# Transposing activations by VectorE blocks and DRAM instead of by TensorE, in a two-block transformer kernel

## The chip, the cores and the metric

The kernel runs as one program on 1 core of a Trainium2 chip. The metric is device time of one execution in microseconds (us). Before the change three timed runs gave a median of 2368.16 us (2367.35 to 2370.7). The profile is of one further execution of the same program.

## The reference

Two transformer blocks in a row over 256 tokens of width 2048, all in float32. The first has differential attention, an indexed sparse attention and a gated feed-forward layer; the second has latent attention beside a gated convolution. What matters here:

```python
# first block, feed-forward (D_FF = 5632)
ff = (jax.nn.silu(h @ w_gate) * (h @ w_up)) @ w_down

# second block
proj = h @ w_in_2      # split into q_a, c_kv, k_rope, z_mla, c_in, b_gate, c_gate, z_conv, g_mla, g_conv
attn = attn * jax.nn.silu(z_mla)
y_mla = attn @ w_o_mla
u = c_gate * c_in
conv = sum(conv_w[k] * u_pad[:, k:k + s] for k in range(3))       # along the tokens
y_conv = (b_gate * conv * jax.nn.silu(z_conv)) @ w_o_conv
merged = jax.nn.sigmoid(g_mla) * y_mla + jax.nn.sigmoid(g_conv) * y_conv
out = merged @ w_out
```

Each product that is multiplied by a further matrix (the feed-forward product, the gated attention, the gated convolution and the merged sum) comes out of TensorE with tokens on the partitions. The next matmul needs it with channels on the partitions, so it has to be transposed; the convolution runs along the tokens and is computed on the transposed `u`.

## The kernel before, in words

Tokens are two tiles of 128 (t = 0, 1). A weight matrix is taken in groups of up to 512 columns (`Grp`), a group in units of two 128-row pieces (`kc`). Every float32 operand is split exactly in two parts (hi and lo), and TensorE adds three products per piece and token tile: hi by wh, hi by wl, lo by wh (line 65 records each matmul). A group over 16 pieces is 96 matmuls of 128x512.

Weights come by SyncE (SP) in loads of 1 MB, one load for two units, into four buffers `raw`. For each unit ScalarE writes `wh` (line 286) and VectorE writes `wl` (line 287); both have four buffers (`N_SPLIT`), and a unit is split at most three units ahead of the matmuls (`LOOK`). A buffer of `raw` is free again when both of its units are split, and the next load is issued right behind that split.

The order on every engine is the order in which the Python program emits instructions; each engine runs its own list in that order and stops at the first instruction whose inputs are not there. When the last matmul of a group for one t is emitted, `spawn` starts a generator `post_...`, which empties the PSUM bank. A generator gives up control with `yield d` and is taken up again when the program's own clock, which `PE.matmul` and `PE.transpose` advance, has gone on by d us (4.84 where nothing is given); that clock is a means of placing instructions and no measurement.

For a transpose, `quad_transpose` emits four TensorE transposes of 128x128 into one PSUM bank (line 70), and `put_quad` then writes the hi part with ScalarE (line 549) and the lo part with VectorE (line 550). It is used behind the feed-forward product (`post_up`, tile `act`), for `u` (`post_cgate`), for the gated convolution (`post_bgate`, tile `m`), for the gated attention (`post_z`, tiles `at`) and for the merged sum (`post_omla`, tiles `thm`). Each goes once per group and token tile.

The framework gives every DMA one of eight completion semaphores in turn (`DMAHW0` to `DMAHW7`); before SP issues a DMA it waits until the DMA eight places earlier has landed, where that is not known already.

Of the kernel before, what the change touches and what calls it, by code (L numbers as in the profile page):

```python
# [9 lines left out]
F32 = mybir.dt.float32  # L10
# [3 lines left out]
AF = mybir.ActivationFunctionType  # L14
# [3 lines left out]
P = 128  # L18
# [21 lines left out]
def kernel(ctx: ExitStack, tc: tile.TileContext, a, freq, out):  # L40
    nc = tc.nc
# [10 lines left out]
    drp = ctx.enter_context(tc.tile_pool(name="drp", bufs=1, space=bass.MemoryType.DRAM))  # L52
    ctx.enter_context(tc.manual_schedule())

    V, A, G = nc.vector, nc.scalar, nc.gpsimd
# [15 lines left out]

    T = PE

    # ------------------------------------------------------------------ storage
    slots = deque(range(14))
    slot_of = {}

# [12 lines left out]
    def wtile(shape=(P, 512), dt=F32, tag="w", bufs=4, name="w"):  # L90
        return wk.tile(list(shape), dt, name=name, tag=tag, bufs=bufs)
# [27 lines left out]
    def sc_bank():  # L119
        return psx.tile([P, 512], F32, name="sc", tag="sc", bufs=2)  # L120

    # ------------------------------------------------------------------ driver
    bg = []
    H = {}

# [246 lines left out]
                t = tt  # L372
            stages[-j](items[i])

    # ------------------------------------------------------------------ constants
    v1 = wtile(tag="P", bufs=4, name="v1")
    v1 = v1[:, :P]
    rows = lambda v, n: v.rearrange("o (r c) -> (o r) c", c=P)[:n]
# [30 lines left out]
    pb = tp_bank()  # L409
# [94 lines left out]
        V.tensor_scalar(nlam, nlam, 0.2, None, op0=OP.subtract)  # L504


    # ------------------------------------------------------------------ helpers
    def rstd_of(ssq, n, width, name="rstd"):
        k = ssq.shape[1]
        v = small(k, name + "v")  # L510
# [10 lines left out]
    def quad_transpose(src, pb=None):  # L521
        pb = pb if pb is not None else tp_bank()
        n = src.shape[1] // P
        for j in range(n):
            T.transpose(pb[:, j * P:(j + 1) * P], src[:, j * P:(j + 1) * P], ident)
        return pb[:, :n * P].rearrange("p (c q) -> p c q", q=P)
# [16 lines left out]
    def put_quad(pair, q, t, src, scale=None):  # L543
        hi, lo = pair
        k = 4 * q
        h = hi[k // 8][:, k % 8:k % 8 + 4, t * P:(t + 1) * P]
        l = lo[k // 8][:, k % 8:k % 8 + 4, t * P:(t + 1) * P]
        if scale is None:
            A.activation(h, src, AF.Copy)
            V.tensor_sub(l, src, h)  # L550
        else:
            A.activation(h, src, AF.Copy, scale=scale)
            V.scalar_tensor_tensor(l, src, scale, h, op0=OP.mult, op1=OP.subtract)

    # ------------------------------------------------------------------ modulation
    def ada_item(load, use, after=lambda: None):
        return {"kind": "ada", "item": {"kind": "ada", "load": load, "use": use}, "after": after}

# [3 lines left out]
    hid = {}  # L562
# [154 lines left out]
                set_state("ada_free", True)  # L717
        return gen

    # ------------------------------------------------------------------ first norm  # L720
    ssx = cst.tile([P, 2, 4], F32, name="ssx")
    first = ada_chunk(0)
    firsts = []
# [7 lines left out]
    for t in range(2):  # L731
# [5 lines left out]
        r = rstd_of(sum4(ssx[:, t, :]), 1, D)  # L737
        for q in range(4):
            xs = x_t[t][:, 512 * q:512 * (q + 1)]
            V.tensor_scalar(xs, xs, r, None, op0=OP.mult)  # L740
            pb = quad_transpose(xs)
            d = nT[q // 2][:, 4 * (q % 2):4 * (q % 2) + 4, t * P:(t + 1) * P]
# [6 lines left out]
    free("x0", "x1", "ada0", "ada1", "ada2", "ada3")  # L749
    hid["hi"], hid["lo"] = [big("h1h0", dt=R32), None], [big("h1l0", dt=R32), None]  # L750

    # ------------------------------------------------------------------ w_in of the first block
    acc = {}
    for q in range(2):
        acc["A", q] = big(f"accA{q}", (P, 2, 2, 512))
# [12 lines left out]
    w_in = a["w_in"][0]  # L768
# [26 lines left out]
            s += g.steps()  # L795
        return s

    # index scores and the selection of keys
    iws = cst.tile([P, 2, 16], F32, name="iws")

    def idx_gen():
# [310 lines left out]
    sd.insert(nd, call(start_diff))  # L1112
    steps += merge(sd, gate_a + shift_f)

    # ------------------------------------------------------------------ output of the attention
    mix_hi = lambda kc, t: (hid["mh%d" % (kc // 8)][:, kc % 8, t * P:(t + 1) * P],
                            hid["ml%d" % (kc // 8)][:, kc % 8, t * P:(t + 1) * P])
    w_o = a["w_o"][0]
# [91 lines left out]
    def after_o():  # L1210
        free("mh0", "ml0", "mh1", "ml1")

    # ------------------------------------------------------------------ feed-forward
    DFF = 5632
    w_gate, w_up, w_down = a["w_gate"][0], a["w_up"][0], a["w_down"][0]
    lhs2 = lambda kc, t: hilo_lhs(*hid["h2"])(kc, t)
# [4 lines left out]
    def post_gate(g):  # L1221
        def post(t, ps):
            sil[t] = hold("sil")
            A.activation(sil[t], ps, AF.Silu)
            yield 0
        return post

    def post_up(g, q):
        def post(t, ps):
            w = wtile(name="act")  # L1230
            V.tensor_mul(w, ps, sil[t])
            yield
            put_quad(hid["act"], q, t, quad_transpose(w))
        return post

    def act_alloc():
# [62 lines left out]
    for p, (g0, ng) in enumerate(parts):  # L1299
        if p == 0:  # L1300
            fsteps.append(call(after_o))
        fsteps.append(call(act_alloc))
        for g in range(g0, g0 + ng):
            if g == 1:
                fsteps.append(call(rel_mo))
            for nm, w, post in (("gate", w_gate, post_gate(g)), ("up", w_up, post_up(g, g - g0))):
                fsteps += Grp(f"{nm}{g}", w, 512 * g, 512, range(16), lhs2, post,
                              need=lambda ks, t: [f"h2.{t}.{k // 4}" for k in ks],
                              begin=2 if nm + str(g) == "gate0" else 1).steps()
        for g in range(4):  # L1310
            post = post_down(g, p) if p < 2 else post_norm_in(ffacc, ssf, g, "Gf", fin_f)

            def need(ks, t, p=p, g0=g0):
                r = [f"up{k // 4}.{t}" for k in ks]
                return r + (["ada5"] if p == 2 else [])
            fsteps += Grp(f"down{p}_{g}", w_down, 512 * g, 512, range(4 * g0, 4 * (g0 + ng)), lhs_act(p),
                          post, need=need, end=3 if (p, g) == (2, 3) else 1).steps()
# [2 lines left out]

    steps += fsteps[nf:]

    # ------------------------------------------------------------------ second block
    w_in2 = a["w_in_2"]
    lhs3 = lambda kc, t: hilo_lhs(*hid["h3"])(kc, t)
    need3 = lambda ks, t: [f"h3.{t}.{k // 4}" for k in ks]
# [58 lines left out]
    steps += Grp("ck0", w_in2, 512, 288, range(16), lhs3, post_ck0).steps()  # L1385
    steps += Grp("ck1", w_in2, 800, 288, range(16), lhs3, post_ck1).steps()

    # gated convolution
    C_IN, B_GATE, C_GATE, Z_CONV = 3136, 5184, 7232, 9280
    G_MLA, G_CONV, Z_MLA = 11328, 13376, 1088  # L1390
    uT = {}
# [10 lines left out]
    def post_cgate(g):  # L1402
        def post(t, ps):
            w = wtile(name="u")
            V.scalar_tensor_tensor(w, ps, r3[:, t, 0:1], sil[t], op0=OP.mult, op1=OP.mult)
            yield
            if g not in uT:
                uT[g] = big(f"uT{g}", (P, 2, 4, 256))
            u = uT[g]
            A.activation(u[:, 0, :, t * P:(t + 1) * P], quad_transpose(w), AF.Copy)  # L1410
            yield
            if t == 1:
                for j in range(4):
                    k = 4 * g + j
                    V.tensor_scalar(u[:, 1, j, :], u[:, 0, j, :], col2[:, 48 + k:49 + k], None, op0=OP.mult)
                    V.scalar_tensor_tensor(u[:, 1, j, 1:256], u[:, 0, j, 0:255], col2[:, 32 + k:33 + k],
                                           u[:, 1, j, 1:256], op0=OP.mult, op1=OP.add)
                    V.scalar_tensor_tensor(u[:, 1, j, 2:256], u[:, 0, j, 0:254], col2[:, 16 + k:17 + k],
                                           u[:, 1, j, 2:256], op0=OP.mult, op1=OP.add)
                    yield  # L1420
        return post
# [6 lines left out]
    def post_bgate(g):  # L1428
        def post(t, ps):
            w = wtile(name="m")  # L1430
            V.scalar_tensor_tensor(w, ps, r3[:, t, 0:1], sil[t], op0=OP.mult, op1=OP.mult)
            yield
            while not done(f"cgate{g}.0", f"cgate{g}.1"):
                yield POLL
            pb = quad_transpose(w)
            y = wtile(name="yc")
            y3 = y.rearrange("p (c q) -> p c q", q=P)
            V.tensor_mul(y3, pb, uT[g][:, 1, :, t * P:(t + 1) * P])
            put_quad(hid["y"], g, t, y3)
            yield 0  # L1440
            if t == 1:
                free(f"uT{g}")
        return post
# [8 lines left out]
    yc = [None, None]  # L1452
# [14 lines left out]
        steps += Grp(f"oconv{g}", a["w_o_conv_2"], 512 * g, 512, range(16), lhs_y, post_oconv(g),  # L1467
                     need=lambda ks, t: [f"bgate{k // 4}.{t}" for k in ks]).steps()

    # latent attention  # L1470
    knT, vt, qnT = [None, None], [None, None], [None, None]

    def kv_alloc():
# [140 lines left out]
    def post_z(g):  # L1614
        def post(t, ps):
            th = wtile(name="thz")
            A.activation(th, ps, AF.Tanh, scale=r3[:, t, 1:2])
            V.scalar_tensor_tensor(th, th, 1.0, ps, op0=OP.add, op1=OP.mult)
            yield 0
            if "att" not in hid:  # L1620
                while not done("mla"):
                    yield POLL
                if "att" not in hid:
                    hid["att"] = mk_pair("att")
            d = at[t][:, 512 * g:512 * (g + 1)]
            V.scalar_tensor_tensor(d, d, r3[:, t, 1:2], th, op0=OP.mult, op1=OP.mult)
            yield
            put_quad(hid["att"], g, t, quad_transpose(d))
        return post

    gsteps = []
# [29 lines left out]
    def post_omla(g):  # L1661
        def post(t, ps):
            d = thm[t][:, 512 * g:512 * (g + 1)]
            V.scalar_tensor_tensor(d, d, 1.0, ps, op0=OP.add, op1=OP.mult)
            V.tensor_add(d, d, yc[t][:, 512 * g:512 * (g + 1)])
            yield
            put_quad(hid["mer"], g, t, quad_transpose(d), 0.5)
        return post

    lhs_att = lambda kc, t: hilo_lhs(*hid["att"])(kc, t)  # L1670
# [2 lines left out]
    for g in range(4):  # L1673
        steps += Grp(f"omla{g}", a["w_o_mla_2"], 512 * g, 512, range(16), lhs_att, post_omla(g)).steps()

    # output projection
    ot = [None, None]
    x2 = [None, None]
    ssz = cst.tile([P, 2, 4], F32, name="ssz")
# [72 lines left out]
```

## Time and profile before

| | us |
|---|---|
| timed runs, median (lowest to highest) | 2368.16 (2367.35 to 2370.7) |
| profiled execution, span from the first to the last instruction | 2365.9 |
| TensorE matmul busy | 2315.8 (98%) |
| VectorE busy | 1306.1 (55%) |
| ScalarE busy | 1069.0 (45%) |
| bytes moved | 506.57 MB, 214 GB/s over the span |

The profiled execution's span lies 2.3 us under the median of the timed runs; what lies around the span is within that difference. A span is cut into 40 equal slices on the page, and a digit gives a slice's busy share in tenths. "busy" of TensorE's matmuls is modelled from their starts, so that a stream of them shows as 100% while each is listed with a duration longer than its distance to the next. The name before `<-` is the tile that is written, the names behind it are those that are read.

### The profile page before, as it was taken

How to read it: one execution, taken by the hardware profiler on the slowest of the kernel's cores; microseconds unless marked ns; L12 is line 12 of the kernel's file. 1: busy time of each engine (PE TensorE's matmuls, PEld its weight loads, DVE VectorE, ACT ScalarE, POOL GpSimd, SP SyncE). 2: the span in 40 equal slices, each digit the busy share in tenths (PEclk: the TensorE clock that was granted, in tenths of full speed). 3: DMA queues.
4: the chain of work that ended last, by engine and by line, in shares of the span. 5: the costliest groups of instructions: out<-in, count | busy, mean ns of one | idle time of the engine just before them, and what ended most of it. 6: DMA issues, size and time to landing. Idle time of an engine off the chain costs nothing.

```text
span 2365.9 us, 27898 instructions
## 1 busy us (share of the span) xinstructions
PE 2315.8 (98%) x11044; PEld 1842.3 (78%) x11044; DVE 1306.1 (55%) x1710; ACT 1069.0 (45%) x1503; POOL 96.8 (4%) x117
## 2 busy tenths in 40 slices
PE   7999999999999999999998999999999999999998
PEld 5666666677887888888887888888888988888887
DVE  3656756556664444554556655555544654554554
ACT  4434345546444444434444644444445544444443
POOL 1311011010000000000001000000000000000000
PEclk9999999999999999999999999999999999999999
DMA  9996888957775556556554665565565553565563
GB/s 302 330 320 237 318 309 301 318 209 277 242 261 191 191 192 195 179 196 195 186 188 144 220 195 190 179 200 188 179 204 161 168 171 125 172 219 196 187 204 125
DMA packets 237619, 506.57 MB, mean 214 GB/s; under 512 B 9288, under 2 KB 31984, under 8 KB 228400
## 3 DMA queue, kind: packets, MB, share of 16 engines
q1 hardware_dynamic: 235392, 496.14, 62.3%
q0 software_dynamic: 1872, 8.58, 1.1%
q8 instruction: 86, 1.41, 0.2%
q14 instruction: 45, 0.37, 0.0%
q10 hardware_dynamic: 224, 0.07, 0.0%
HBM read 500.56 MB, written 4.19 MB: 213 GB/s over the span
## 4 chain that ended last, share of the span: by engine, by line
PE 75%; DVE 1%; ACT 1%; issue 1%; POOL 0%; DVEq 0%; POOLq 0%; ACTq 0%
PE mm L65 71%; PE tp L70 1%; PE sc L65 1%; PE tp L65 1%; PE tpb L70 1%; DVE wl L287 0%; DVE xr L1155 0%; ACT h3h L1163 0%; DVE h3l L1166 0%; POOL rstd L513 0%; ACT wh L286 0%; ACT junk L1178 0%; DVE ot L1705 0%; ACT hm L1277 0%; DVE hm L1273 0%
## 5 line engine op out<-in xcount | busy, mean ns | idle before, releaser
L287 DVE TENSOR_TENSOR wl<-raw,wh 128x1024 fp32r<-128x1024 f32 (+3 forms) x723 | 871.9, 1212 | 766.5 <-ACT wh L286 760.4
L286 ACT ACTIVATE wh<-raw 128x1024 fp32r<-128x1024 f32 (+3 forms) x723 | 745.9, 1038 | 696.4 <-PE mm L65 686.3
L65 PE MATMUL mm<-wh,h3h 128*128 128x512 f32 (+1 forms) x992 | 387.1, 390 | 1.7 <-ACT h3h L1163 1.2
L65 PE MATMUL mm<-wl,h3h 128*128 128x512 f32 (+1 forms) x992 | 380.7, 384 | 0.4 <-DVE wl L287 0.4
L65 PE MATMUL mm<-wh,h3l 128*128 128x512 f32 (+1 forms) x992 | 381.0, 384 | 0.0
L65 PE MATMUL mm<-wh,h2h 128*128 128x512 f32 x704 | 276.3, 393 | 0.0
L65 PE MATMUL mm<-wl,h2h 128*128 128x512 f32 x704 | 274.6, 390 | 0.9 <-DVE wl L287 0.9
L65 PE MATMUL mm<-wh,h2l 128*128 128x512 f32 x704 | 274.7, 390 | 0.0
L65 PEld LDWEIGHTS mm<-wh,h3h 128*128 128x128 f32 x992 | 186.7, 188 | 37.8 <-ACT h3h L1163 1.6
L65 PEld LDWEIGHTS mm<-wh,h3l 128*128 128x128 f32 x992 | 186.5, 188 | 37.4 <-DVE h3l L1166 0.4
L65 PEld LDWEIGHTS mm<-wl,h3h 128*128 128x128 f32 x992 | 186.8, 188 | 34.8 <-DVE wl L287 0.6
L65 PE MATMUL mm<-wh,h1h 128*128 128x512 f32 (+2 forms) x384 | 154.0, 401 | 3.4 <-ACT wh L286 2.5
L65 PEld LDWEIGHTS mm<-wl,h2h 128*128 128x128 f32 x704 | 132.5, 188 | 28.1 <-DVE wl L287 1.2
L65 PEld LDWEIGHTS mm<-wh,h2h 128*128 128x128 f32 x704 | 132.5, 188 | 27.7 <-issue 0.8
L65 PEld LDWEIGHTS mm<-wh,h2l 128*128 128x128 f32 x704 | 132.4, 188 | 27.6
L65 PE MATMUL mm<-wl,h1h 128*128 128x512 f32 (+2 forms) x384 | 142.7, 372 | 7.8 <-DVE wl L287 7.8
L65 PE MATMUL mm<-wh,h1l 128*128 128x512 f32 (+2 forms) x384 | 142.0, 370 | 1.9 <-DVE h1l L627 1.9
L65 PE MATMUL mm<-wh,acth 128*128 128x512 f32 x352 | 139.3, 396 | 0.0
L65 PE MATMUL mm<-wh,actl 128*128 128x512 f32 x352 | 137.1, 390 | 0.0
L65 PE MATMUL mm<-wl,acth 128*128 128x512 f32 x352 | 137.0, 389 | 0.0
L65 PEld LDWEIGHTS mm<-wh,h1h 128*128 128x128 f32 x384 | 72.8, 190 | 55.7 <-issue 26.7
L65 PEld LDWEIGHTS mm<-wl,h1h 128*128 128x128 f32 x384 | 72.9, 190 | 21.2 <-DVE wl L287 10.9
(412 smaller groups left out, 2777.7 us busy)
## 6 DMA issues: line engine op xcount, KB each, us to landing
raw<-in_w_in_dram SPq DMA_DIRECT2D x134, 1024.0 KB, 5.2
raw<-in_w_ada_dram SPq DMA_DIRECT2D x47, 1024.0 KB, 4.9
raw<-in_w_gate_dram SPq DMA_DIRECT2D x44, 1024.0 KB, 5.3
raw<-in_w_up_dram SPq DMA_DIRECT2D x44, 1024.0 KB, 5.2
raw<-in_w_down_dram SPq DMA_DIRECT2D x44, 1024.0 KB, 5.1
raw<-in_w_ada_dram SPq DMA_DIRECT2D x36, 512.0 KB, 8.9
rawb<-in_w_ada_dram SPq DMA_DIRECT2D x17, 1024.0 KB, 6.5
raw<-in_w_o_conv_dram SPq DMA_DIRECT2D x16, 1024.0 KB, 5.1
```

Of the source, the lines that this page charges most:

```text
L65: return nc.tensor.matmul(o, l, r, **kw)
L70: return nc.tensor.transpose(o, i, idn)
L286: A.activation(wh[:, :m, :g.n], src, AF.Copy)
L287: V.tensor_sub(wl[:, :m, :g.n], src, wh[:, :m, :g.n])
```

## The change

A helper `flip_quad` takes the place of `quad_transpose` in 21 groups for both token tiles, 42 times: 8 of the 11 feed-forward groups (all but the last of each of the three parts), the four `u` groups, three of four `m` groups, three of four `at` groups and three of four `thm` groups. In each, VectorE transposes the 128x512 tile within 32x32 blocks into `scr`; four DMAs, one for each 32 partitions, write `scr` to a DRAM buffer in runs of 32 elements (128 bytes); one DMA reads the buffer back with 128 contiguous elements (512 bytes) per run, channels on the partitions. The result `fm` (or `uT` itself) lies in SBUF, and `put_quad` reads it there. All these DMAs are issued by SP. The generator gives up control for 2 us behind the block transpose, and for 8 us (`FLIP`) behind the writes and again behind the read.

```diff
+    FLIP = 8.0
+    n_flip = [0]
+
+    def flip_quad(src, dst=None):
+        n_flip[0] += 1
+        dr = drp.tile([P, 512], F32, name=f"flip{n_flip[0]}")
+        scr = wtile(tag="PT", bufs=2, name="scr")
+        V.transpose(scr, src)
+        yield 2.0
+        for i in range(4):
+            d = bass.AP(tensor=dr.tensor, offset=dr.offset + 32 * i, ap=[[P, 32], [32 * P, 16], [1, 32]])
+            nc.sync.dma_start(d, scr[32 * i:32 * i + 32].rearrange("p (b r) -> p b r", r=32))
+        yield FLIP
+        if dst is None:
+            dst = wtile(tag="P", bufs=4, name="fm").rearrange("p (c q) -> p c q", q=P)
+        s = bass.AP(tensor=dr.tensor, offset=dr.offset, ap=[[P, P], [P * P, 4], [1, P]])
+        nc.sync.dma_start(dst, s)
+        yield FLIP
+        return dst
...
-    def post_up(g, q):
+    def post_up(g, q, last):
         def post(t, ps):
             w = wtile(name="act")
             V.tensor_mul(w, ps, sil[t])
-            yield
-            put_quad(hid["act"], q, t, quad_transpose(w))
+            if q < last:
+                m3 = yield from flip_quad(w)
+            else:
+                yield
+                m3 = quad_transpose(w)
+            put_quad(hid["act"], q, t, m3)
         return post
...
             u = uT[g]
-            A.activation(u[:, 0, :, t * P:(t + 1) * P], quad_transpose(w), AF.Copy)
-            yield
+            yield from flip_quad(w, u[:, 0, :, t * P:(t + 1) * P])
...
-            pb = quad_transpose(w)
-            y = wtile(name="yc")
-            y3 = y.rearrange("p (c q) -> p c q", q=P)
-            V.tensor_mul(y3, pb, uT[g][:, 1, :, t * P:(t + 1) * P])
+            if g < 3:
+                y3 = yield from flip_quad(w)
+                V.tensor_mul(y3, y3, uT[g][:, 1, :, t * P:(t + 1) * P])
+            else:
+                pb = quad_transpose(w)
+                y = wtile(name="yc")
+                y3 = y.rearrange("p (c q) -> p c q", q=P)
+                V.tensor_mul(y3, pb, uT[g][:, 1, :, t * P:(t + 1) * P])
```

`post_z` (for g of 1 to 3) and `post_omla` (for g of 0 to 2) get the same two branches as `post_up`.

SyncE at the end of the feed-forward group up4, before the change: only weight loads follow one another, each waiting for the split that frees its buffer (`DVE_49`).

```order
L262 DMA raw_6750<-in_w_gate_dram 128x4x512 [waits DMAHW5_49,DVE_49]
L262 DMA raw_6784<-in_w_up_dram 128x4x512 [waits DMAHW6_49,DVE_49]
L262 DMA raw_6817<-in_w_up_dram 128x4x512 [waits DMAHW7_49,DVE_49]
L262 DMA raw_6872<-in_w_up_dram 128x4x512 [waits DMAHW0_49,DVE_49]
L262 DMA raw_6906<-in_w_up_dram 128x4x512 [waits DMAHW1_49,DVE_49]
```

SyncE at the same place after the change (`flip7` is the DRAM buffer of t = 0, `flip8` that of t = 1, `scr` the block-transposed tile, `fm` the tile read back):

```order
L262 DMA raw_6808<-in_w_up_dram 128x4x512 [waits DMAHW4_49,DVE_49]
L262 DMA raw_6847<-in_w_up_dram 128x4x512 [waits DMAHW5_49,DVE_49]
L566 DMA flip7_6822<-scr_6823 32x16x32 x4
L566 DMA flip8_6833<-scr_6834 32x16x32 [waits DMAHW6_49]
L566 DMA flip8_6833<-scr_6834 32x16x32 [waits DMAHW7_49]
L566 DMA flip8_6833<-scr_6834 32x16x32 [waits DMAHW0_49]
L566 DMA flip8_6833<-scr_6834 32x16x32 [waits DMAHW1_49]
L262 DMA raw_6896<-in_w_up_dram 128x4x512 [waits DMAHW2_49,DVE_49]
L571 DMA fm_6904<-flip7_6822 128x4x128 [waits DMAHW5_49,DMAHW4_49,DMAHW3_49]
L571 DMA fm_6916<-flip8_6833 128x4x128 [waits DMAHW6_49,DMAHW7_49,DMAHW1_49,DMAHW0_49]
L262 DMA raw_6934<-in_w_up_dram 128x4x512 [waits DVE_49]
```

Ten DMAs have come between three weight loads. The four writes of `flip8` wait for the four weight loads before them, the last of these for `raw_6847`, which SP has just issued. Each read waits for the writes of its own buffer, and the load `raw_6934` stands behind both reads.

ScalarE at the same place before the change: the two copies of the transposed product, each waiting for TensorE, stand among the splits.

```order
L286 ACTIVATE wh_6792<-raw_6675 128x1024 [waits DMAHW7_49,DVE_49,PE_49]
L286 ACTIVATE wh_6813<-raw_6675 128x1024 [waits DVE_49,PE_49]
L549 ACTIVATE acth0_4641<-tp_6832 128x4x128 [waits PE_49]
L286 ACTIVATE wh_6845<-raw_6716 128x1024 [waits DMAHW0_49,DVE_49]
L549 ACTIVATE acth0_4641<-tp_6849 128x4x128 [waits PE_49]
L286 ACTIVATE wh_6868<-raw_6716 128x1024 [waits DVE_49]
```

ScalarE after the change, from the same split on (`wh_6843` is now what `wh_6813` was, the second unit of its load):

```order
L286 ACTIVATE wh_6843<-raw_6699 128x1024 [waits DVE_49,PE_49]
L286 ACTIVATE wh_6876<-raw_6740 128x1024 [waits DMAHW6_49,DVE_49,PE_49]
L286 ACTIVATE wh_6892<-raw_6740 128x1024 [waits DVE_49,PE_49]
L286 ACTIVATE wh_6912<-raw_6774 128x1024 [waits DMAHW7_49,DVE_49,PE_49]
L286 ACTIVATE wh_6930<-raw_6774 128x1024 [waits DVE_49,PE_49]
L286 ACTIVATE wh_6948<-raw_6808 128x1024 [waits DMAHW0_49,DVE_49,PE_49]
L286 ACTIVATE wh_6964<-raw_6808 128x1024 [waits DVE_49,PE_49]
L549 ACTIVATE acth0_4641<-fm_6904 128x4x128 [waits DMAHW3_49]
L549 ACTIVATE acth0_4641<-fm_6916 128x4x128 [waits DMAHW4_49]
L286 ACTIVATE wh_6980<-raw_6847 128x1024 [waits DMAHW1_49,DVE_49,PE_49]
```

The copies stand six splits later than before, and wait for the landing of the two reads instead of for TensorE.

## Rows read from the trace of the kernel before

**Rows 1.** The page, sections 1 and 2: busy us (share) xinstructions; digits are tenths per slice.
```profile
PE 2315.8 (98%) x11044; PEld 1842.3 (78%) x11044; DVE 1306.1 (55%) x1710; ACT 1069.0 (45%) x1503; POOL 96.8 (4%) x117
...
PEclk9999999999999999999999999999999999999999
DMA  9996888957775556556554665565565553565563
```

**Rows 2.** Busy time by stretch: PE, PEld, DVE, ACT, POOL, granted clock, DMA share, GB/s.
```profile
590.00:710.00 120.00, 120.00 (x542) 99.40 (x542) 77.63 (x64) 51.82 (x55) 0.00 (x0) 1.00 0.73 252
710.00:1230.00 520.00, 520.00 (x2322) 428.22 (x2321) 254.85 (x229) 219.83 (x230) 0.00 (x0) 1.00 0.58 191
1380.00:1720.00 340.00, 340.00 (x1533) 281.63 (x1532) 190.13 (x203) 145.93 (x152) 0.00 (x0) 1.00 0.58 189
2030.00:2110.00 80.00, 80.00 (x366) 66.26 (x365) 47.88 (x49) 37.50 (x42) 1.12 (x2) 1.00 0.63 212
2180.00:2260.00 80.00, 80.00 (x366) 66.28 (x365) 45.65 (x46) 33.83 (x36) 0.37 (x1) 1.00 0.57 187
```

**Rows 3.** TensorE in order of time around one pair: start, duration, instruction.
```profile
909.02 0.39 PE L65 MATMUL mm<-wh,h2h 128*128 128x512 f32 x1
909.25 0.39 PE L65 MATMUL mm<-wl,h2h 128*128 128x512 f32 x1
909.48 0.40 PE L65 MATMUL mm<-wh,h2l 128*128 128x512 f32 x1
909.71 0.60 PE L70 MATMUL tpb<-ident,act 128*128 128x128 f32 x4
910.07 0.47 PE L65 MATMUL mm<-wh,h2h 128*128 128x512 f32 x1
910.38 0.39 PE L65 MATMUL mm<-wl,h2h 128*128 128x512 f32 x1
910.61 0.40 PE L65 MATMUL mm<-wh,h2l 128*128 128x512 f32 x1
```

**Rows 4.** Instructions on tile act: count, duration min/median/max, first and last start.
```profile
L70 PE MATMUL tp<-ident,act x72: 270/272/275, 595.5 to 1221.2; 128*128 128x128 f32 x72
...
L70 PE MATMUL tpb<-ident,act x16: 270/272/275, 909.7 to 1176.8; 128*128 128x128 f32 x16
```

**Rows 5.** ScalarE in order of time around group up4; in brackets idle before, and releaser.
```profile
861.36 1.06 ACT L286 ACTIVATE wh<-raw 128x1024 fp32r<-128x1024 f32 x1 [1.66 <-PE mm L65]
865.88 0.60 ACT L549 ACTIVATE acth<-tp 128x512 fp32r<-128x512 f32 x1 [3.47 <-PE tp L70]
...
870.46 1.06 ACT L286 ACTIVATE wh<-raw 128x1024 fp32r<-128x1024 f32 x1 [1.21 <-PE mm L65]
873.18 1.06 ACT L286 ACTIVATE wh<-raw 128x1024 fp32r<-128x1024 f32 x1 [1.66 <-PE mm L65]
```

**Rows 6.** VectorE in order of time, same place.
```profile
860.87 1.28 DVE L1231 TENSOR_TENSOR act<-mm,sil 128x512 f32<-128x512 f32 x2
862.45 1.23 DVE L287 TENSOR_TENSOR wl<-raw,wh 128x1024 fp32r<-128x1024 f32 x1 [0.30 <-ACT wh L286]
```

**Rows 7.** VectorE groups by shape: count, busy us, mean ns, idle before.
```profile
L550 DVE TENSOR_TENSOR actl<-tp,acth 128x512 fp32r<-128x512 f32 x18 | 12.4, 687 | 21.7 <-ACT acth L549 21.7
L550 DVE TENSOR_TENSOR yl<-yc,yh 128x512 fp32r<-128x512 f32 x8 | 5.5, 692 | 5.6 <-ACT yh L549 5.6
L1514 DVE COPY qrT<-tp 128x128 f32<-128x128 f32 x11 | 2.9, 281 | 0.0
L287 DVE TENSOR_TENSOR wl<-raw,wh 128x1024 fp32r<-128x1024 f32 x677 | 833.3, 1236 | 739.0 <-ACT wh L286 733.0 <-PE mm L65 4.3
```

**Rows 8.** SyncE's waits, whole span: us in total, times, longest.
```profile
SPq L262 <- DVE wl L287: 1593.1, 323, 14.3
```

**Rows 9.** DMA issues: count, KB each, median us to landing.
```profile
raw<-in_w_up_dram SPq DMA_DIRECT2D x44, 1024.0 KB, 5.2
out_dram<-ot SPq DMA_DIRECT2D x8, 256.0 KB, 2.1
```

**Rows 10.** The page, section 3, whole span: packets, MB, share of 16 engines.
```profile
q1 hardware_dynamic: 235392, 496.14, 62.3%
```

**Rows 11.** The same of 0 to 20 us: ScalarE's small loads.
```profile
q10 hardware_dynamic: 224, 0.07, 1.4%
```

**Rows 12.** SyncE's issue of one weight load: start, duration.
```profile
858.26 0.37 SPq L262 DMA_DIRECT2D raw<-in_w_up_dram  x1
```

More of the change, by code (lines that the diff above doesn't have):

```diff
@@ L1305 @@
                 fsteps.append(call(rel_mo))
-            for nm, w, post in (("gate", w_gate, post_gate(g)), ("up", w_up, post_up(g, g - g0))):
+            for nm, w, post in (("gate", w_gate, post_gate(g)), ("up", w_up, post_up(g, g - g0, ng - 1))):
                 fsteps += Grp(f"{nm}{g}", w, 512 * g, 512, range(16), lhs2, post,
@@ L1626, in post @@
             V.scalar_tensor_tensor(d, d, r3[:, t, 1:2], th, op0=OP.mult, op1=OP.mult)
-            yield
-            put_quad(hid["att"], g, t, quad_transpose(d))
+            if g:
+                m3 = yield from flip_quad(d)
+            else:
+                yield
+                m3 = quad_transpose(d)
+            put_quad(hid["att"], g, t, m3)
         return post
@@ L1665, in post @@
             V.tensor_add(d, d, yc[t][:, 512 * g:512 * (g + 1)])
-            yield
-            put_quad(hid["mer"], g, t, quad_transpose(d), 0.5)
+            if g < 3:
+                m3 = yield from flip_quad(d)
+            else:
+                yield
+                m3 = quad_transpose(d)
+            put_quad(hid["mer"], g, t, m3, 0.5)
         return post
```

## The prediction

> **What bounds the kernel now.** I read the page's busy shares first: TensorE 98%, the next engine 55%, the granted clock at full speed in all 40 slices [rows 1]. A share over the span hides stages, so I asked for the stretches in which the 42 transposes of the change lie. In all five TensorE is busy for the whole stretch (520.00 of 520 us, 340.00 of 340 us and so on), at a granted clock of 1.00, the level of 2.4 GHz, while VectorE is at 49 to 65%, ScalarE at 42 to 47% and the DMA engines at 0.57 to 0.73 [rows 2]. There TensorE sets the end, and nothing else is near it. SyncE waits for VectorE's splits to free a weight buffer, 323 times for 1593.1 us [rows 8]: weights wait for buffers, not buffers for weights. ScalarE's splits wait for TensorE in turn [rows 5], which closes the loop: TensorE is the pacemaker, and the engines behind it have room.
>
> **What goes from TensorE.** 42 quads of transposes, 168 instructions. Their listed duration, 272 ns each [rows 4], is not the price, because TensorE overlaps them. The price is read from starts. In a stream of matmuls one starts every 0.227 us (909.02, 909.25, 909.48). From 909.48 the third matmul further on would start at 909.48 + 3 x 0.227 = 910.16; with the quad between it starts at 910.61 [rows 3]. One quad costs 0.45 us, and 42 cost 18.9 us. All 42 lie in stretches in which TensorE never rests, so the whole sum is on the path. From the same rows, the bounds of a quad: 0.60 us (the quad's own listed time) and 0.36 us (910.07 less 909.71, without the slower restart), so 15 to 25 us for all; I take 0.45.
>
> **What comes on VectorE.** 42 block transposes of 128x512 from SBUF. The trace has none. Bounds: 0.28 us (copy of 128x128) and 1.24 us (two-input operation of 128x1024) [rows 7]; I take 0.7, as the two-input operations of 128x512 have. That makes 29 us on an engine that idles 739 us before the wl splits alone [rows 7]. The lo parts are now read from SBUF instead of PSUM: 692 ns against 687 [rows 7], nothing. On the path this counts only if a wl comes late. TensorE uses a unit three units after its buffer is freed: a unit is 2.72 us (870.46 to 873.18), so 8.2 us later, and the split takes 1.06 us on ScalarE and 1.23 on VectorE [rows 5, 6]. That leaves 5.8 us of room, and the added 1.4 us per pair fit. The cover is real: in this kernel ScalarE is already held 3.47 us at each first quad [rows 5], and TensorE does not rest there [rows 2].
>
> **What comes on SyncE and DMA.** Per pair (t = 0 and 1) eight writes and two reads, 210 issues in all at 0.37 us [rows 12]: 3.7 us per pair, in an interval of 5.4 us between two loads. Packets per pair: 8 x 512 of 128 bytes and 2 x 512 of 512 bytes. No row shows packets of 128 bytes, or a write in such runs. Bounds: a packet of 2 KB takes 0.623 x 16 x 2365.9 / 235392 us = 100 ns [rows 10], so 6 ns if only bytes count and 100 ns if only packets count. The nearest row has 300 bytes in the mean: 0.014 x 16 x 20 / 224 us = 20 ns [rows 11]. I take 20: on each of 16 engines 256 x 20 = 5.1 us for the writes and 64 x 20 = 1.3 us for the reads. The Trainium skill speaks against the change here ("DMA: Bandwidth & Descriptors", Specifications): runs under 512 bytes do not reach line rate, since the engine reads, modifies and writes. If that doubles the write, an estimate by that page, it is 40 ns and 10.2 us per pair; no run so far shows it, and by the following working the sum would not change.
>
> **Is the round trip in time?** This is where the forecast stands or falls, since ScalarE works in order and `acth<-fm` stands in front of the next split. I follow up4 on the old trace. The products are made from 860.87 to 862.15 [rows 6]; with two block transposes the next wl ends near 864.8, and then SP issues `raw_6847`, which lands at 870.0 (5.2 us [rows 9]). The first four writes queue behind it. The fourth write of `flip8` may only be issued once that load has landed, 870. The load's own data are through by about 868, then 5.1 us of writes: 873 to 874, and landed near 875. `raw_6896` follows at 870.5, behind the writes, its data (512 packets of 2 KB, 3.2 us) done by 877; the second read follows at 875, its data done by 878 and landed near 879. ScalarE, after six more splits of 2.72 us from 861.36, comes to the copy at 878.7. So it is held some 0.3 us, of 5.8 that are free. Price if the cover is gone: every microsecond of hold beyond 5.8 is one of TensorE, per pair. That happens from 5.5 us more on 256 packets, 41 ns a packet. In the convolution `u` is transposed one yield later and read by VectorE; by the same steps the reads land about 5 us before their use. The weight loads: `raw_6896` is half a microsecond late, `raw_6934` waits for the second read until 875.4 and would have been issued at about 875.7 anyway. The four buffers hold some 15 us of work beyond that, so this costs nothing.
>
> DMA share: 8 loads per 43.5 us (two groups of 96 x 0.227) keep the engines at 0.58; a pair adds 6.4 us, 0.15. In the at and thm stretches a pair comes every 21.8 us, adding 0.29 to 0.57 or 0.63 [rows 2]: 0.92 at most, for three groups in a row. In the first stretch (0.73) it becomes 0.88. Under 1 everywhere.
>
> **Sum.** 18.9 us off a span of 2365.9 gives 2347.0; with the 2.3 us by which the median of the runs shown exceeds that span, 2349.3 us.
>
> **Rivals.**
>
> *Held copies.* Packets near 43 ns, or landings of the writes some 6 us longer than I have: ScalarE holds each of the 14 tight pairs (8 feed-forward, 3 at, 3 thm) about half a microsecond beyond its room, 7 us in all: 2356. For it: my margin is a few microseconds of queueing that I stacked by hand. Against it: in the convolution the room is larger, and a hold of 3.47 us shows no cost now.
>
> *No change.* The time given up by TensorE is taken by the next bound at once, between 2364 and 2373. For it: the DMA engines come to 0.9 in places. Against it: VectorE and ScalarE are under two thirds [rows 2], and SP waits 1593.1 us [rows 8]. The version in which the transposes were hidden anyway is excluded by the 0.45 us in rows 3.
>
> *Slower: the 128-byte writes choke the queue.* All loads and flips share one in-order SP queue and the same 16 engines. At 60 ns a packet the writes of a pair take 15.4 us, 10.2 more than assumed; the copy is held 10.5 us, 4.7 beyond the room; 14 pairs give 66 us, less 18.9: about 2415. At the upper bound of 100 ns the hold is 20.8 us, 15 beyond the room, and the convolution's seven pairs pass theirs as well by some 10 us: above 2600. The point from which it decides is where the loss per pair passes 18.9 / 14 = 1.35 us: 47 ns a packet. For it: no row shows such writes to DRAM. Against it: the row at 300 bytes shows 20 ns. The rule of the Trainium skill named above (same page and section) is what would make it true; at twice the row it stops short of that point, as worked out above.
>
> **How the numbers follow.** Forecast, the whole sum with little loss (2345 to 2353): 0.68. Held copies (2353 to 2362): 0.14. No change: 0.06. Slower: 0.12. 0.2% is 4.7 us, about what a measurement of this kernel can tell from no change. Faster is the first two, 0.82; the same 0.06; slower 0.12. Likeliest 2349.3. The range reaches down to 2345 (25 us would be the upper bound of the quads, but rows 3 show the restart in it) and up to 2364, over all of the held copies; the choked queue and most of no change stay outside, under 2 in 10.
>
> **What would show it.** In the profile of the changed kernel: TensorE busy for the whole of the feed-forward, convolution, at and thm stretches, and 168 fewer transposes; a STREAM_TRANSPOSE on `scr` near 0.7 us; the flip writes at 2 to 10 us to landing and the reads at 3 to 6; idle time before `acth<-fm` small, in any case under 5.8 us, with no wait of TensorE for `wh` or `wl` behind it; DMA share in rows like rows 2 about 0.15 and 0.3 higher. I am wrong if TensorE shows gaps of a microsecond or more some 20 us behind the end of a group, or if SP's waits for DMA come near its waits for VectorE.

## The result, and the profile after

The changed kernel takes 2349.24 us (median of 4 runs, 2348.06 to 2350.41), the kernel before 2368.83 in the same comparison (4 runs): a ratio of 0.9921, 95% interval 0.9908 to 0.9935. That is 19.6 us less by the medians. The profiled execution has a span of 2347.4 us against 2365.9, so 18.5 us less.

First the page of the changed kernel, section 1 (busy us, share, instructions), and section 3 (packets, MB, share of 16 engines):

```profile
PE 2295.9 (98%) x10876; PEld 1824.8 (78%) x10876; DVE 1331.7 (57%) x1752; ACT 1066.2 (45%) x1495; POOL 96.8 (4%) x117
...
q1 hardware_dynamic: 346272, 518.18, 67.6%
```

Against [rows 1], TensorE has 168 instructions fewer and 19.9 us less busy time; VectorE has 42 more and 25.6 us more. Against [rows 10], SP's queue has 110,880 more packets.

The five stretches of [rows 2], at the places to which they have moved, in the same columns:

```profile
590.00:705.00 115.00, 115.00 (x509) 95.20 (x509) 77.87 (x68) 50.62 (x54) 0.00 (x0) 1.00 0.88 282
705.00:1222.00 517.00, 517.00 (x2289) 425.84 (x2288) 264.27 (x241) 221.51 (x231) 0.00 (x0) 1.00 0.63 204
1372.00:1705.00 333.00, 333.00 (x1475) 275.74 (x1474) 198.11 (x217) 142.39 (x144) 0.00 (x0) 1.00 0.72 215
2014.00:2094.00 80.00, 80.00 (x358) 66.34 (x357) 51.53 (x54) 38.46 (x42) 1.11 (x2) 1.00 0.76 229
2163.00:2243.00 80.00, 80.00 (x355) 66.24 (x354) 50.30 (x52) 34.25 (x35) 0.53 (x1) 1.00 0.72 216
```

TensorE still never rests in them, at a granted clock of 1.00. The DMA share has grown, and VectorE's busy time by the block transposes.

Now the round trip of group up4, on SP in order of time (start, duration, instruction):

```profile
861.87 7.67 SPq L566 DMA_DIRECT2D flip<-scr  x8
869.64 0.45 SPq L262 DMA_DIRECT2D raw<-in_w_up_dram  x1
870.20 1.36 SPq L571 DMA_DIRECT2D fm<-flip  x2
```

and ScalarE behind it (in brackets the idle time before, and what ended it):

```profile
874.37 1.06 ACT L286 ACTIVATE wh<-raw 128x1024 fp32r<-128x1024 f32 x1 [1.66 <-PE mm L65]
875.96 0.63 ACT L549 ACTIVATE acth<-fm 128x512 fp32r<-128x512 f32 x1 [0.52 <-DMA fm<-flip]
```

Eight writes are issued in 7.67 us, the reads at 870.2, and the first has landed at 875.9, 0.52 us after ScalarE was ready for it. Before, ScalarE stood 3.47 us here for TensorE [rows 5]. The sums of such waits in the changed kernel (us in total, times, longest), of ScalarE for the reads:

```profile
ACT atth L549 <- DMA fm<-flip: 11.3, 6, 7.2
...
ACT acth L549 <- DMA fm<-flip: 8.0, 9, 2.6
ACT merh L552 <- DMA fm<-flip: 6.8, 6, 3.7
```

and of TensorE for the splits, which in the kernel before came to 9.0 and 2.5 us:

```profile
PE mm L65 <- DVE wl L287: 10.0, 10, 2.7
...
PE mm L65 <- ACT wh L286: 3.1, 3, 2.1
```

ScalarE is held 26 us in all, and TensorE's waits for the splits grow by 1.6. I call such a wait of ScalarE a hold; there are 14 pairs in which one can matter (8 feed-forward, 3 at, 3 thm).

### The profile page after: what moved, and what is told of

It reads as the page before. It is cut to its first block, busy times and chain, and to the rows that moved or that the text cites. A ratio compares the mean times of both kernels' runs of the same rounds, so it can differ in the third digit from the quotient of the medians.

```text
span 2347.4 us, 27890 instructions
## 1 busy us (share of the span) xinstructions
PE 2295.9 (98%) x10876; PEld 1824.8 (78%) x10876; DVE 1331.7 (57%) x1752; ACT 1066.2 (45%) x1495; POOL 96.8 (4%) x117
## 3 DMA queue, kind: packets, MB, share of 16 engines
q1 hardware_dynamic: 346272, 518.18, 67.6%
q0 software_dynamic: 1872, 8.58, 1.1%
## 4 chain that ended last, share of the span: by engine, by line
PE 73%; DVE 2%; ACT 1%; DMA 1%; issue 1%; SPq 0%; POOL 0%; DVEq 0%; POOLq 0%; ACTq 0%
PE mm L65 70%; PE sc L65 1%; PE tp L65 1%; DMA fm<-flip 1%; PE tp L70 1%; DVE wl L287 0%; SPq L566 0%; PE tpb L70 0%; ACT wh L286 0%; DVE xr L1175 0%; ACT h3h L1183 0%; DVE h3l L1186 0%; POOL rstd L513 0%; ACT junk L1198 0%; DVE ot L1740 0%
```

## The experiments

The theory: the change gives 42 x 0.45 us of TensorE back, and holds cost nothing until they pass the room that the splits have. The rivals: the gain has another source, any hold costs its length, or the queue with its small writes is near its limit. All ratios are to the kernel before, run beside each experiment on the same chip (2367.3 to 2367.7 us). Where I give a *loss* of TensorE behind a hold, it is the time by which its starts lie further apart than 0.227 us (starts over 0.3 us apart counted), from 4 to 24 us after ScalarE arrived at the copy; over the 14 holds of the changed kernel it is 2.6 us, of which 0.9 is there without a hold too (runs 7 and 8).

**1. The quads back on TensorE, unused.** An addition to the changed kernel:

```
-        yield FLIP
+        yield 2.84
+        quad_transpose(src)
+        yield FLIP - 2.84
```

> Added to the changed kernel: each of the 42 flips also has its four TensorE transposes made as in the kernel before, into a PSUM bank that nobody reads. Theory (the gain is TensorE time): 42 x 0.45 = 18.9 us come back, so about 2368 us, the time of the kernel before. Rival (the gain comes from ScalarE's hi copies no longer waiting for a transposed quad): stays near 2349. Half way, 2358, would mean that a quad costs TensorE half of what the starts showed.

Measured: 2374.41 us, 1.0030 (1.0017 to 1.0042). The starts on TensorE:

```profile
908.22 0.40 PE L65 MATMUL mm<-wh,h2l 128*128 128x512 f32 x1
908.45 0.60 PE L70 MATMUL tpb<-ident,act 128*128 128x128 f32 x4
908.81 0.47 PE L65 MATMUL mm<-wh,h2h 128*128 128x512 f32 x1
909.12 0.39 PE L65 MATMUL mm<-wl,h2h 128*128 128x512 f32 x1
909.35 0.40 PE L65 MATMUL mm<-wh,h2l 128*128 128x512 f32 x1
```

The third matmul behind 908.22 would start at 908.90 and starts at 909.35: 0.45 us, as in [rows 3]. The whole gain is gone, which excludes ScalarE's shorter wait as its source. It went further than expected, by 6 us: the quads also shifted the schedule, so that copies stand 1.7 to 3.1 us earlier behind their block transposes. The third hold of at grew from 7.2 to 9.6 us, that of thm from 3.7 to 7.9, and the loss behind the holds from 2.6 to 10.8. 18.9 + 8.2 = 27.1 us, and the spans differ by 27.1; some 0.7 us of restarts behind quads is in both terms, so the sum closes to within 1 us.

**2 and 3. Copies earlier.** `FLIP = 6.0`, and `FLIP = 4.0`, in place of 8.0.

> FLIP 6.0 instead of 8.0: each read is issued, and each copy stands, one step earlier twice over, about 4 us in all. Theory (a copy may be held some 6.3 us before TensorE notices): the holds of after (0 to 2.6 us in the feed-forward, 1 to 7 in at and thm) grow by up to 4 us, and only those that pass 6.3 us cost; summed over the 14 tight pairs 6 to 7 us, so about 2355 (2349 to 2358). Rival (any hold costs TensorE its full length): 14 pairs x 4 us, 2400 and more. Rival (reads wait for the writes, not for their place in the order, and nothing is late): 2349.

Measured: 2377.42 us, 1.0047 (1.0034 to 1.0059): slower than before, and 22 us above what I expected.

> FLIP 4.0: the same two steps, 8 us earlier in all. Theory (room 6.3 us): holds of 8 to 15 us, less up to 3 us by which the reads, issued ahead of one load more, land earlier; 14 pairs lose 1 to 3.3 us each, so 2365 to 2395, the gain gone. If the holds cost nothing: 2349. The step from FLIP 6 to FLIP 4 should be several times that from 8 to 6, since the room is used up between them.

Measured: 2385.64 us, 1.0078 (1.0065 to 1.0091). Within the range, but not as a whole: the second step costs 8 us and the first 28, where I expected the second to be the larger.

With FLIP 6 the feed-forward's copies stand two units of 2.72 us earlier, 11.7 us behind the block transpose instead of 17.1, while the reads land when they did. Two holds of the FLIP 6 kernel, in up4 and in the second at group (ScalarE):

```profile
882.33 0.63 ACT L549 ACTIVATE acth<-fm 128x512 fp32r<-128x512 f32 x1 [6.50 <-DMA fm<-flip]
...
2083.42 0.63 ACT L549 ACTIVATE atth<-fm 128x512 fp32r<-128x512 f32 x1 [9.98 <-DMA fm<-flip]
```

The first costs TensorE 0.5 us; holds of 4.6, 5.0 and 6.0 in the same stage cost nothing. So the feed-forward's room is about 6.0 us, near the 5.8 of the prediction and the 6.3 I had corrected it to. The first holds of at and thm give the same (6.76 with a loss of 0.79, 6.58 with 0.63). The second hold above costs 6.6 us, far more than 9.98 less 6.0, and the windows behind it say why (columns as in [rows 2]):

```profile
2070.00:2082.80 12.80, 12.80 (x58) 10.62 (x57) 3.54 (x4) 1.79 (x2) 0.00 (x0) 1.00 0.95 251
2085.90:2092.40 6.50, 6.03 (x13) 4.43 (x14) 6.39 (x8) 4.08 (x6) 0.22 (x1) 0.50 0.47 156
2092.90:2100.00 7.10, 7.10 (x33) 5.85 (x32) 5.04 (x5) 2.54 (x3) 0.53 (x1) 1.00 0.92 336
```

TensorE stood from 2083 to 2085.9, and then the granted clock was 0.50, the level of 1.2 GHz, for these 6.5 us: 13 matmuls, where 6.5 / 0.227 = 28 would fit. The idle time is paid, and then some of it again. Over the 14 pairs the loss is 28.6 us, 26.0 more than in the changed kernel; the spans differ by 27.0. The theory of a free room holds; my expected sum was too small, since I took 4 us for a shift of 5.4 and no clock into it. With FLIP 4 the copies stand another two units earlier, but the reads, now ahead of a load in SP's queue, land mostly 3 to 4 us earlier too, so the holds grow little: 120 us in all against 102. There the copies of at and thm stand well ahead of the next group's end. The first hold of at, on ScalarE:

```profile
2066.11 0.63 ACT L549 ACTIVATE atth<-fm 128x512 fp32r<-128x512 f32 x1 [8.29 <-DMA fm<-flip]
```

and VectorE behind it:

```profile
2069.47 4.68 DVE L287 TENSOR_TENSOR wl<-raw,wh 128x1024 fp32r<-128x1024 f32 x4
2074.07 0.68 DVE L1645 SCALAR_TENSOR_TENSOR thz<-thz,mm 128x512 f32<-128x512 f32 x1
```

The wl splits that were held are worked off before the next group's product comes at 2074.07. This hold costs 1.4 us, and so do the second of at and the first two of thm, 8.2 to 8.3 us each: a room of 6.8 us, as in the feed-forward of this run (holds of 6.7 and 6.9 cost nothing, 7.8 and 7.9 cost 0.9 and 1.1).

**4, 5 and 6. More writes.** Added behind each flip's writes of the changed kernel, in three forms; `spare` is a buffer in DRAM that nobody reads. Every write a second time:

```
+        for i in range(4):
+            ...
+            nc.sync.dma_start(d, scr[32 * i:32 * i + 32].rearrange("p (b r) -> p b r", r=32))
```

> Added to the changed kernel: each flip's four block writes are made once more, to a buffer in DRAM that nobody reads, so 42 x 2048 more packets of 128 bytes. At the 13 ns a packet that the changed kernel's trace has, a pair adds 256 x 13 ns = 3.4 us on each DMA engine. Theory (room): the holds grow by about 3.4 us, to 3 to 6 us in the feed-forward, under the room of 6.3; at and thm, where three holds were 2.4, 3.7 and 7.2, lose about 4 us: 2349 to 2357. Rival of the prediction (writes of 128 bytes choke the queue, here because their count is doubled): 14 pairs x 3.4 us, 2397 or more.

Measured: 2389.67 us, 1.0101 (1.0087 to 1.0115). Much worse than the theory gave, near the rival. So I took the issues and the packets apart:

```
+            nc.sync.dma_start(dx[32 * i:32 * i + 32, 0:1], scr[32 * i:32 * i + 32, 0:1])
```

> Added to the changed kernel: four more writes per flip of 32 values of 4 bytes each, which nobody reads: the same number of additional issues on SP as in the run with every write made twice, with nearly no transfer time (128 packets of 4 bytes against 2048 of 128). That run was 40 us slower than the changed kernel. If SP's issues and the places in the queue made that (8 x 0.37 = 3 us more per pair before the reads can go out), this one is slower by a similar 25 to 40 us, about 2374 to 2390. If the packets made it, this one stays near 2349 to 2355.

Measured: 2386.78 us, 1.0083 (1.0070 to 1.0097). And all packets in one issue:

```
+        d = bass.AP(tensor=dx.tensor, offset=dx.offset, ap=[[1024, P], [64, 16], [1, 32]])
+        nc.sync.dma_start(d, scr.rearrange("p (b r) -> p b r", r=32))
```

> Added to the changed kernel: one more write per flip of 2048 packets of 128 bytes, which nobody reads: the packets of the doubled writes in one issue instead of four. If the packets made the 40 us of that run (256 x 13 ns = 3.4 us more per pair on each DMA engine), this one is slower by 25 to 40 us too. If the issues did, it stays under 2355. If they add up, the two differences from 2349 sum to about 40.

Measured: 2380.28 us, 1.0055 (1.0043 to 1.0068). Neither of my two readings holds alone, and they don't add up: 37 and 31 us one by one, 40 together. What they share is that the reads land later. SP in the run with four small issues, at up4:

```profile
870.73 2.61 SPq L566 DMA_DIRECT2D flip<-scr  x4
873.38 4.59 SPq L569 DMA_DIRECT2D spare<-scr  x4
878.02 2.06 SPq L566 DMA_DIRECT2D flip<-scr  x4
880.12 1.89 SPq L569 DMA_DIRECT2D spare<-scr  x4
882.11 0.39 SPq L262 DMA_DIRECT2D raw<-in_w_up_dram  x1
882.54 1.05 SPq L574 DMA_DIRECT2D fm<-flip  x2
```

Four writes of 128 bytes each hold SP as long as four of 64 KB, or longer. From the block transpose to the landing of the first read it is 17.6 us at up4 in the changed kernel, 21.8 here, 21.2 with the packets alone and 22.6 with both. Yet the five holds of 870 to 1222 us, all of 2.4 to 5.5 us in these three runs, cost TensorE nothing. The loss is in the first stretch, and above all in at and thm. There it comes at holds under 6.0 us. Behind the 14 pairs it grows by 45.5, 36.6 and 29.4 us in runs 4, 5 and 6, the spans by 48.0, 37.2 and 30.8 (the profiled execution of run 4 took 2397.2 us, more than the median above). So nearly all of the price lies behind the copies, though in the first stretch ScalarE waits for weight loads too, 21 to 24 us from 590 to 720 us against 5.1 in the changed kernel. One of the holds of the small-issue run, on ScalarE:

```profile
2064.31 0.63 ACT L549 ACTIVATE atth<-fm 128x512 fp32r<-128x512 f32 x1 [5.58 <-DMA fm<-flip]
```

VectorE in order of time behind it:

```profile
2066.78 1.23 DVE L287 TENSOR_TENSOR wl<-raw,wh 128x1024 fp32r<-128x1024 f32 x1 [0.26 <-ACT wh L286]
2067.92 0.68 DVE L1648 SCALAR_TENSOR_TENSOR thz<-thz,mm 128x512 f32<-128x512 f32 x1
2068.64 0.75 DVE L1656 SCALAR_TENSOR_TENSOR at<-at,r,thz 128x512 f32<-128x512 f32 x1
2069.43 0.71 DVE L562 STREAM_TRANSPOSE scr<-at 128x512 f32<-128x512 f32 x1
2070.06 0.65 DVE L1648 SCALAR_TENSOR_TENSOR thz<-thz,mm 128x512 f32<-128x512 f32 x1
2070.74 0.75 DVE L1656 SCALAR_TENSOR_TENSOR at<-at,r,thz 128x512 f32<-128x512 f32 x1
2071.53 0.71 DVE L562 STREAM_TRANSPOSE scr<-at 128x512 f32<-128x512 f32 x1
2072.16 4.59 DVE L287 TENSOR_TENSOR wl<-raw,wh 128x1024 fp32r<-128x1024 f32 x4
```

and TensorE:

```profile
2071.06 0.39 PE L65 MATMUL mm<-wh,h3h 128*128 128x512 f32 x1
2073.40 0.67 PE L65 MATMUL mm<-wl,h3h 128*128 128x512 f32 x1 [1.95 <-DVE wl L287]
2073.86 0.63 PE L65 MATMUL mm<-wh,h3l 128*128 128x512 f32 x1
```

Here a group ends every 21.8 us, so the copy that stands 16 to 17 us behind one group's block transpose comes just before the next group's end. The backlog of wl splits that the hold left should be worked off then; instead 4.2 us of the next group's work, two block transposes among it, stand in front of it. The hold of 5.58 costs 3.7 us, since the next eight starts behind the gap are 0.43 to 0.46 us apart, at a granted clock of 0.53 (2073.4 to 2076.0).

**7. Another queue.** The flips' writes and reads with `nc.gpsimd.dma_start` in place of `nc.sync.dma_start`.

> The changed kernel with the flips' writes and reads issued by GpSimd on its own DMA queue instead of SP's. Theory (a write is late because it stands behind a load of 1 MB in SP's queue, issue blocked up to 4 us): the writes land earlier, the holds of ScalarE (24 us in sum over 14 pairs, two over 3.6) vanish, and the 2 to 3 us that two of them cost TensorE come back: 2346 to 2348. Rival (the transfers are set by the 16 engines that all queues share, and GpSimd's issues cost more): holds as before or longer, 2349 to 2380.

Measured: 2347.98 us, 0.9916 (0.9903 to 0.9930). GpSimd, and ScalarE, at up4:

```profile
860.30 5.18 POOL L566 DMA_DIRECT2D flip<-scr  x8 [164.00 <-DVE scr L562]
868.81 0.79 POOL L571 DMA_DIRECT2D fm<-flip  x1 [3.33 <-ACT wh L286]
```

```profile
875.38 1.06 ACT L286 ACTIVATE wh<-raw 128x1024 fp32r<-128x1024 f32 x1 [1.66 <-PE mm L65]
876.35 1.14 ACT L549 ACTIVATE acth<-fm 128x512 fp32r<-128x512 f32 x2
```

The eight writes are issued in 5.18 us instead of 7.67, ScalarE waits for no first read of a pair any more (for second ones 3.4 us in all, 1.5 at most), and the loss behind the pairs falls from 2.6 to 0.9 us. As expected in the trace; that the kernel is faster than the changed one is not shown, since the intervals of the two times overlap.

**8. Copies later.** `FLIP = 10.0`.

> FLIP 10.0: reads and copies later, by one or two units of 2.7 us each; by the order of ScalarE the two copies of a pair now stand one split apart. Theory (what is left to gain is what the longest holds, 7.2 and 3.7 us, cost): no hold over 6 us, the gaps of TensorE in the at and thm stretches go, 2.6 us less, about 2346.5 (2345 to 2349). Rival (later copies come late for the down projections or the next stage): 2350 to 2360.

Measured: 2348.25 us, 0.9918 (0.9904 to 0.9931); the sum of first holds falls from 23.7 to 2.4 us, the loss from 2.6 to 0.9, and the span is 2345.4, 2.0 less. The same answer as run 7, by time instead of by speed; here too the intervals overlap with the changed kernel's.

**9. Doubled writes with later copies.** Run 4 with `FLIP = 10.0`.

> Every flip's four writes made twice, as in the run of 2390 us, but with FLIP 10.0, so that the copies stand some 5 us later. Theory (held copies are the whole price of late transfers): the reads land 22 to 27 us after the block transpose and the copies now stand at 19 to 22, so holds of 0 to 6 us with the loss in two or three pairs alone: 2349 to 2358. Rival (the doubled writes also make the weight loads late, or the queue itself is the bound): 2370 to 2390, as with FLIP 8.

Measured: 2360.12 us, 0.9967 (0.9956 to 0.9979). 30 of the 40 us are back, with the same packets and issues. So most of their price was held copies, not the queue. Of the 11 us that remain, 5.9 are loss behind the 14 pairs, most of it behind two holds of 6.9 and 9.4 in the third at and thm groups. Nearly all of the rest lies in the first stretch, where the rival has its part. ScalarE waits for weight loads (us in total, times, longest):

```profile
ACT wh L286 <- DMA raw<-in_w_up_dram: 33.0, 6, 9.6
```

In the changed kernel it is 5.1. From 590 to 720 us TensorE's starts lose 6.4 us here and 0.7 there, nearly all of it outside the counts of the pairs: where the DMA engines are busiest (0.87 here), the doubled writes do make weight loads late.

**10. Two quads more.** Run 7, with `if True:` for `if g:` in `post_z`.

> The version with the flips on GpSimd's queue (2348.0), and the two quads of the at stage's first group, which the changed kernel leaves on TensorE, flipped as well. Theory (0.45 us a quad, no holds): 2348.0 - 0.9 = 2347.1. Rival (these two are needed earlier than the others, or collide with the end of the latent attention): 2349 or more.

Measured: 2347.72 us, 0.9915 (0.9901 to 0.9928). The span is 0.7 us less than in run 7. The sign is as expected, but such a step is below what the runs can tell.

**11. The feed-forward alone.** `A.activation` and `quad_transpose` as before in the convolution, and `if False:` for the tests in the at, thm and b_gate groups.

> Only the 16 quads of the feed-forward are flipped, the other 26 stay on TensorE. Theory (every quad that goes is worth 0.45 us wherever it stands): 16 x 0.45 = 7.2 us less than before, about 2361. Rival (the gain comes from one stage or one collision, not from the count): at 2349 or at 2368.

Measured: 2360.93 us, 0.9973 (0.9964 to 0.9981), so 4.5 to 8.5 us less than before; 7.2 expected. A quad has the same worth here as over all, as far as the interval tells (0.28 to 0.53 us).

**12. Block transposes twice.** `V.transpose(scr, src)` written two times.

> Every block transpose made twice into the same tile, so 42 x 0.71 = 30 us more of VectorE. Theory (VectorE's part is hidden in the feed-forward and the convolution; it counts where a hold is already long, by delaying the writes 0.7 to 1.4 us and by standing in front of wl): 1 to 6 us, from the pairs of at and thm alone, 2350 to 2355. Rival (VectorE's added time is on the path): 30 us, 2379.

Measured: 2362.09 us, 0.9976 (0.9967 to 0.9985): 13 us of the added 30, more than the 1 to 6 expected, far less than the rival's 30. Three of its stretches:

```profile
705.00:1222.00 517.00, 517.00 (x2289) 425.70 (x2288) 273.17 (x252) 222.41 (x232) 0.00 (x0) 1.00 0.63 205
1372.00:1705.00 333.00, 333.00 (x1474) 275.75 (x1473) 208.00 (x231) 142.53 (x145) 0.00 (x0) 1.00 0.69 215
2014.00:2094.00 80.00, 77.51 (x338) 63.45 (x337) 53.38 (x58) 36.04 (x40) 1.12 (x2) 0.98 0.70 221
```

In the feed-forward and the convolution the 8.9 and 9.9 us more of VectorE are wholly hidden; in at TensorE idles 2.5 us and the granted clock falls (0.59 from 2088 to 2092). Behind a hold of only 4.43 us 4.1 us are lost there. The loss behind the 14 pairs grows by 12.8 us, the span by 13.5. Here holds and added VectorE work come together, as under run 5.

## Why the prediction was right, and where not

**TensorE's part**: right. 0.45 us a quad is what the trace of run 1 shows again, and with its longer holds counted the sum of 42 closes to within 1 us; the 16 of run 11 agree within their interval. Of 18.9 us predicted off the span, 18.5 came; without holds the spans were 0.7 (run 7) and 2.0 us (run 8) shorter, which is within the 2.4 us by which the spans of the changed kernel's own executions differ.

**VectorE's part**: the size is right, and the cover holds only in part. Of the changed kernel's 42 block transposes 28 last as those of the feed-forward do, the 14 of the convolution 703 ns:

```profile
L562 DVE STREAM_TRANSPOSE scr<-act x16: 711/711/712, 591.4 to 1165.2; 128x512 f32<-128x512 f32 x16
```

(nanoseconds, minimum, median and maximum; 0.7 us taken). Hidden they are in the feed-forward and the convolution, whatever was done to them. In at and thm the room of 5.8 us that I worked out at up4 does not hold where the next group's end follows the copy within some 5 us (runs 5 and 12); with the copies well ahead of that end it does (run 3). The changed kernel's own holds there, 0.95 and 2.42 us, 0.94 and 1.51 in the first two pairs of each, stay inside what is left. The third of at, 7.18, has no such VectorE work of a next group behind it and loses 1.1 us. The third of thm, 3.67, has 2.7 us of the last group's products in front of the splits, and TensorE's next transposes wait 0.43 us for them; 0.8 us are lost, of which 0.2 is there without a hold (run 7).

**Packets**: too dear. I had 21 x 6.4 = 134 us on each engine; the share of SP's queue grows from 62.3% of 2365.9 [rows 10] to 67.6% of 2347.4, which is 113 us. The packets of 128 bytes last 13.2 ns in the mean by the trace's packet records, not 20; those of 512 bytes 28.8. The row that I took 20 from [rows 11] has no packet near its mean of 300 bytes: by the records it is 128 packets of 512 bytes at 28.1 ns and 96 of 4 bytes at 9.0. The rule of the Trainium skill that I had weighed ("DMA: Bandwidth & Descriptors", Specifications), that runs under 512 bytes miss line rate since the engine reads, modifies and writes, agrees with the trace in kind: 13.2 ns is twice the 6 ns that 128 bytes would take at the rate of the packets of 2 KB. That a second pass is the cause is not shown: packets of 4 bytes on SP's queue last 9.1 ns, so a fixed part in each packet would explain it as well. The 40 ns that I had worked out by that rule are three times what was measured.

**The round trip**: right at the pair I followed, and not by all of its steps. I had the read landing 0.3 us after ScalarE came; it was 0.52. The writes' data were faster than I had it, but SP was held longer in issuing them (506 ns each at the median, up to 4151). I followed one pair of 14. The others have 0 to 2.6 us in the feed-forward; the third of at has 7.18, since its copy stands 14.2 us behind the block transpose instead of 17.1 and its last write went out at 14.3 instead of 10.7. The convolution's reads land 4.0 to 6.4 us before their use, about as predicted (5).

**DMA share**: 0.88 in the first stretch and 0.72 in the convolution, as worked out (0.88, 0.73). 0.76 and 0.72 in at and thm, under the 0.92 that I allowed for three groups in a row: a pair took 5.4 us of each engine (113 / 21) instead of 6.4, and these windows hold other groups too.

**The slower rival**: its packets of 60 ns did not come (13.2), but its mechanism, copies held by late reads, is real, and the price of that was too low in my working. I put the point from which it decides at 47 ns a packet, 6.9 us more for a pair's writes. Run 6 delays the landing of the reads by some 3.6 us at up4 and is already 13 us slower than before. The failed step is "every microsecond of hold beyond 5.8 is one of TensorE, per pair": in at and thm the cost starts earlier where the next group's work reaches VectorE before the held splits are done, and a longer gap of TensorE is paid a second time at the lower clock. By the 31 us of that run in proportion, a rough estimate, the gain of 18.9 us ends where the reads land about 2 us later. The forecast came out right with less margin than it claimed.

**The signs that I named**: the flip writes take 5.0 us to landing at the median (2.0 to 9.3), the reads 5.8, and no copy to `acth` waits over 2.6 us. SP's weight loads wait 1400.0 us for wl splits, the flips' reads 14.0 us for their writes. One sign of being wrong did show, once: behind the third hold of at two starts of TensorE lie 1.26 us apart (2103.02 and 2104.28).

**Held copies** (2356) did not come with the copies where the change puts them; two units earlier gave 2377 us (run 2), and one unit earlier was not run. **No change** needed a second bound at TensorE's level, and no stretch shows one.

## What to carry to other kernels

Where one engine is busy through, price what is taken from it by the distance of starts, not by listed durations, and count only the stretches in which it never rests. Before moving such work to a round trip through memory, work out the slack at each place where the result is read, above all where groups end in quick succession: the room at one group is not the room at another. A transfer that arrives just in time costs nothing and hides how near the edge is; place the consumer a unit later, or use a queue of its own, when the order is free.

## What the runs showed of the hardware that was not expected

- A small transfer does not make a DMA issue on SP cheap: with writes of 32 values of 4 bytes the four issues took 1.89 to 4.59 us at up4, the four of 64 KB 2.06 to 2.61.
- GpSimd's queue carried the 210 transfers of the flips in far fewer records: its packets rose from 1,872 in the changed kernel to 10,608, while SP's fell from 346,272 to 235,392. Eight issues there take 5.18 us.
- After TensorE had stood from 2083 to 2085.9 in the FLIP 6 run, the granted clock was 0.50 for the 6.5 us that followed, though it worked through nearly all of them; 15 matmuls' worth of time was lost behind the gap itself.
